# One modulation vector per VectorE product: transposed weights in place of accumulated products and folds

## The chip, the cores and the metric

The kernel runs on one core of one Trainium2 chip. The metric is the device time of one execution in microseconds (us). The core has a matrix engine (PE, TensorE), a vector engine (DVE, VectorE), an activation engine (ACT, ScalarE), GpSimd (POOL), a queue engine (SP, SyncE) that here issues nearly all weight loads, and DMA engines that move data between HBM and the on-chip SBUF. Each engine works through its own queue in order; semaphores tie the queues together.

## What is computed

One layer of a hybrid backbone over 256 latent and 256 context tokens of width 2048. Six modulation vectors come from the conditioning vector c, and two of them for the context too:

```python
mod_x = jnp.split((jax.nn.silu(c) @ w_mod[l] + b_mod[l])[:, None, :], 6, axis=-1)
mod_c = jnp.split((jax.nn.silu(c_ctx) @ w_mod[l] + b_mod[l])[None, None, :], 6, axis=-1)
...
x = x + mod_x[2] * merge_branches(o_attn, o_gla, rb, gate_a, gate_b, ...)
x = x + mod_x[5] * conv_ffn(modulate(x, g_ffn[l], mod_x[3], mod_x[4]), ...)
```

`w_mod` is 2048 x 12288 in float32: six parts of 2048 columns. Parts 0 and 1 (shift and scale ahead of the mixers) are needed for latent and context tokens, at the very start. Parts 2, 3, 4 and 5 are needed for the latent tokens alone and later: part 2 gates the mixers' output, 3 and 4 modulate the input of the feed-forward part, 5 gates its output. This case is about those four, 16.8 million products in all.

Around them stand the input projection (2048 x 13344), a windowed attention, a gated linear attention (GLA), two output projections, the merge, `w_out`, and a feed-forward part (FFN) with an up projection to 11264, a convolution, a gate and a down projection.

## The kernel before

**Weights.** All large products go through `proj_nat`, `proj_T` and `proj_pair`. A step of these (a chunk) takes 256 rows by 512 columns of a weight matrix: one load of 512 KB by SP (`load`, line 104) into a buffer `raw`, of which there are seven (pool `wr`); a rounded copy `whi` on ScalarE (line 227) and the remainder `wlo` on VectorE (line 228), with three buffers each; then the matmuls (line 83). So a chunk's split can run up to three chunks ahead of the matmuls that read it, and its load up to seven buffers ahead of the split. `tick()` runs at the head of every chunk. It calls what was deferred (`defer`), a step of GLA or attention (`beside`), and as many background steps (`bg_steps`) as `bg_rate` allows per chunk.

**Parts 0 and 1** are products on PE (`mod_both`): a load of 1 MB `mraw` from `w_mod`, matmuls into `pm`, a transpose, a product with `sel` into `pcol`.

**Parts 2 to 5** are the background steps of `mod_latent` (line 365), done on VectorE beside the weight products. For each part and each block j of 512 outputs there are eight steps. A step loads 256 rows by 512 columns of `w_mod` into a buffer of the same ring `raw` (the load of the next step is issued too), and adds the two products of a row block with its column of silu(c), `ccol`, onto `macc`, 128 x 512:

```python
i0 = V.scalar_tensor_tensor(a[0], raw[:, k, :], ccol[:, kt:kt + 1], a[0],
                            op0=ALU.mult, op1=ALU.add).ins
```

The first of the sixteen products of a block is a `tensor_scalar` (line 387), the other fifteen are line 391. After the eighth step the sums over the 128 partitions are still to be taken: a transpose within 32 x 32 blocks into `mtr` (line 397), a reduction to `mrs` (line 399), and, three chunks later or at a fixed place, a product with `sel` on PE (`pcl`, through `mm_b`, line 95, in float32), four copies of 32 partitions from PSUM (line 407) and the addition of the bias (line 409). `mm_b` ties such a product to the place in PE's order where it is called.

The first call (line 864) makes parts 3, 4 and 2, 96 steps: at 0.3 steps a chunk during the second key block and three value blocks of the GLA branch, 1.6 during the attention's key and value blocks, none during the query blocks and the attention, and 0.52 from the block `RB` through the merge. The second call (line 1190) makes part 5, 32 steps at 0.36 a chunk beside the first six of eleven blocks of the up projection; its `pcl` products are collected in `sums` and placed at the head of a block's first half (`up_banks`) or ahead of the down projection.

**Order.** Within an engine the order of the queue is not simply that of the program: work that waits for nothing moves ahead of work that does. Where the order matters it is tied by hand (`in_order`, no semaphore): the products of `mod_latent` come after the last `wlo`, the first of the second call after the last modulated tile of the FFN's input. The loads are tied to program order only up to `chain.clear()`, at the end of the opening part.

**The opening.** c is loaded as 16 rows of 128 into `crow`, passed through silu (line 126), turned on PE (line 133) and copied to `cS` (line 135) and `ccol` (line 136). `crow`, the rows of the small weight columns (`rows`, line 143, loaded by POOL) and the diagonal tiles `dg` (line 496) share two buffers, tag `t128`.

Of the kernel before, what the change touches and what calls it, by code (L numbers as in the profile page):

```python
# [8 lines left out]
F32 = mybir.dt.float32  # L9
# [3 lines left out]
ALU = mybir.AluOpType  # L13
AX = mybir.AxisListType
PSUM = bass.MemoryType.PSUM

P = 128
D = 2048
T = 256
KT = D // P  # L20
# [10 lines left out]
def layer_kernel(ctx, tc, A, out):  # L31
    nc = tc.nc
    V, S, G, PE = nc.vector, nc.scalar, nc.gpsimd, nc.tensor

    pool = lambda *a, **k: ctx.enter_context(tc.tile_pool(*a, **k))
    cst = pool(name="cst", bufs=1)
    big = pool(name="big", bufs=16)
    wr = pool(name="wr", bufs=7)
    wh = pool(name="wh", bufs=3)
    f2 = pool(name="f2", bufs=1)  # L40
    sm = pool(name="sm", bufs=4)
# [3 lines left out]

    w_in = A["w_in"][0]
    w_mod = A["w_mod"][0]
    F2_BUFS = {"fa": 4, "fb": 4, "fc": 6, "mod": 2}

    def M(name, shape, dt=F32):  # L50
        return big.tile(shape, dt, name=name, tag="M")
# [1 line left out]
    def W2(tag, name, shape, dt=F32):  # L53
        return f2.tile(shape, dt, name=name, tag=tag, bufs=F2_BUFS[tag])

    def bank(name, shape=(P, 512), side=False):

        return ps.tile(list(shape), F32, name=name, tag="side" if side else "main", bufs=3 if side else 1)
# [5 lines left out]
    def in_order(*ins):  # L64

        for a, b in zip(ins, ins[1:]):
            tc.add_manual_dep(b, a.name, mybir.DependencyInfo(
                mybir.DependencyClass.NoSync, mybir.DependencyReason.DATA), reason="order")
# [25 lines left out]
    def mm_b(*a, **k):  # L94
        return pe_seq(after(PE.matmul(*a, **k)))  # L95
# [6 lines left out]
    def load(dst, src):  # L102

        d = nc.sync.dma_start(dst, src).ins
        if chain and chain[-1] is None:
            chain[:] = [d]
        elif chain:
            tc.add_manual_dep(d, chain[-1].name, mybir.DependencyInfo(
                mybir.DependencyClass.NoSync, mybir.DependencyReason.DATA), reason="order of loads")
            chain[:] = [d]  # L110
        return d
# [16 lines left out]
        S.preload_act_table_set("natural_log_exp_and_others")  # L128
    cS = W2("fb", "cS", [P, KT, 32])
    V.memset(cS, 0.0)  # L130
    ccol = cst.tile([P, KT], F32, name="ccol")
    pt = bank("pc0", (P, 32))
    PE.transpose(pt, crow, ident[:32, :32])
    for i in range(2):
        V.tensor_copy(cS[:, :, i], pt[:, 16 * i:16 * i + 16])
    V.tensor_copy(ccol, pt[:, 0:16])

    def columns(name, parts, eng=G, put=None):
        rows = sm.tile([P, P], F32, name="rows", tag="t128", bufs=2)
# [23 lines left out]
    bg_steps = []  # L163
# [5 lines left out]
    def defer(n, fn):  # L169

        later.append([n, fn])
# [37 lines left out]
    def wload(src):  # L209
        n = src.shape[0] // P  # L210
        raw = wr.tile([P, 2, 512], F32, name="raw", tag="raw")
        load(raw[:, 0:n, :], src.rearrange("(c p) d -> p c d", p=P))
        return raw
# [148 lines left out]
        steps = [lambda k0=k0: step(k0) for k0 in range(0, KT, nk)]  # L362
        return steps if put is not None else steps + [end]

    def mod_latent(parts, put=lambda fn: defer(3, fn), begin=None):


        seq = [(part, dst, j, k0) for part, dst in parts for j in range(4) for k0 in range(0, KT, 2)]
        raws, a = {}, []

        def get(i):
            if i < len(seq) and i not in raws:
                part, _, j, k0 = seq[i]
                c0 = part * D + j * 512
                raws[i] = wload(w_mod[k0 * P:k0 * P + 256, c0:c0 + 512])

        def step(i):
            part, dst, j, k0 = seq[i]
            get(i)
            get(i + 1)  # L380
            if k0 == 0:
                a[:] = [W2("mod", "macc", [P, 512])]
            raw = raws[i]
            for k in range(2):
                kt = k0 + k
                if kt == 0:
                    i0 = V.tensor_scalar(a[0], raw[:, 0, :], ccol[:, 0:1], None, op0=ALU.mult).ins
                    if begin is not None:
                        in_order(begin, i0)
                else:  # L390
                    i0 = V.scalar_tensor_tensor(a[0], raw[:, k, :], ccol[:, kt:kt + 1], a[0],  # L391
                                                op0=ALU.mult, op1=ALU.add).ins
                if k == 0:
                    in_order(last_lo[0], i0)
            if k0 == KT - 2:
                tr = W2("mod", "mtr", [P, 16, 32])
                V.transpose(tr.rearrange("p a c -> p (a c)"), a[0])
                rs = sm.tile([P, 16], F32, name="mrs", tag="mrs", bufs=2)
                V.tensor_reduce(rs, tr, op=ALU.add, axis=AX.X)

                def out():
                    pc = bank("pcl", (32, 16))
                    mm_b(pc, sel[:, 0:32], rs, start=True, stop=True)
                    pv = pc.rearrange("p (a b) -> p b a", b=4)
                    d = dst[:, 4 * j:4 * j + 4]
                    for b4 in range(4):
                        V.tensor_copy(d[32 * b4:32 * b4 + 32, :], pv[:, b4, :])
                    b0 = part * 16 + j * 4
                    V.tensor_tensor(d, d, bmod[:, b0:b0 + 4], op=ALU.add)

                put(out)

        return [lambda i=i: step(i) for i in range(len(seq))]

    def rows_from_cols(name, col):

# [762 lines left out]
    pairs = []  # L1179
# [6 lines left out]
    in_order(pairs[0][0], *[i for kt in range(1, KT) for i in (pairs[kt][0], pairs[kt - 1][1])], pairs[-1][1])  # L1186
    in_order(small[-1], pairs[0][0])
    hold.extend([None, None] + [pairs[2 * c + 1][1] for c in range(2, 8)])
    sums = []
    bg_steps.extend(mod_latent([(5, gcol2)], sums.append, pairs[-1][1]))  # L1190
    bg_rate[:] = [0.36, 0.0]

    def up_banks(side):

        if side == 0:
            while sums:
                defer(3, sums.pop(0))
            return [acc.tile([P, 512], F32, name="acc", tag="acc") for _ in range(4)]
        return [bank("accs", side=(f > 0)) for f in range(4)]

# [2 lines left out]
    for half, blocks in enumerate((range(0, 6), range(6, 11))):  # L1203
        n = len(blocks)
        ah = [M("ah", [P, 8, T], F32R) for _ in range((n + 1) // 2)]
        al = [M("al", [P, 8, T], F32R) for _ in range((n + 1) // 2)]
        for i, j in enumerate(blocks):
            u = [[W2("fc", "u", [P, 2, T]) for _ in range(2)] for _ in range(2)]

            def up_evac(f, b, side, j=j, u=u, i=i, ah=ah, al=al):  # L1210
                p_ = f // 2
                uu = u[side][p_]
                d = uu[:, f % 2, :]
                fi = side * 44 + j * 4 + f
                us = W2("fa", "us", [P, T])
                S.activation(us, b[:, T:2 * T], AF.Copy)
                V.tensor_tensor(us, b[:, 0:T], us, op=ALU.add)
                S.activation(d, us, AF.Identity, scale=cw1[:, fi:fi + 1], bias=cb[:, fi:fi + 1])
                V.scalar_tensor_tensor(d[:, 1:T], us[:, 0:T - 1], cw0[:, fi:fi + 1], d[:, 1:T],
                                       op0=ALU.mult, op1=ALU.add)  # L1220
                V.scalar_tensor_tensor(d[:, 0:T - 1], us[:, 1:T], cw2[:, fi:fi + 1], d[:, 0:T - 1],
                                       op0=ALU.mult, op1=ALU.add)
                if f % 2 == 0:
                    return
                if side == 0:
                    S.activation(uu, uu, AF.Silu)
                else:
                    V.tensor_tensor(uu, uu, u[0][p_], op=ALU.mult)
                    q = slice((i % 2) * 4 + 2 * p_, (i % 2) * 4 + 2 * p_ + 2)
                    split(ah[i // 2][:, q, :], al[i // 2][:, q, :], uu)  # L1230

            for side in range(2):
                proj_pair(w_up, side * DFF + j * 512, ALL, lambda kt: h2[kt // 4][:, kt % 4, :, :],
                          up_banks(side), lambda f, b, side=side: up_evac(f, b, side))
        if half == 0:
            assert not bg_steps
            while sums:
                sums.pop(0)()
            flush()
            gate2 = rows_from_cols("gate2", gcol2)  # L1240
        ends = []
        for j in range(4):
            def dn_evac(t, b, j=j, half=half, gate2=gate2):
                js = slice(j * 512, (j + 1) * 512)
                y = W2("fc", "yd", [P, 512])
                a_ = V.tensor_tensor(y, b, gate2[:, js], op=ALU.mult).ins  # L1246
                if half == 0:
                    V.tensor_tensor(x1[t][:, js], x1[t][:, js], y, op=ALU.add)
                else:
                    if j == 3:  # L1250
                        in_order(*ends, a_)
                    ends[:] = [V.tensor_tensor(y, x1[t][:, js], y, op=ALU.add).ins]  # L1252
                    nc.sync.dma_start(out[0, t * P:(t + 1) * P, js], y)

            proj_nat(w_down, blocks[0] * 512, j * 512, list(range(n * 4)), [tok(ah, al, 0), tok(ah, al, 1)],
                     dn_evac, by_tile=(half == 1 and j == 3))
# [52 lines left out]
```

## Time and profile before

| what | value |
|---|---|
| time before, median of 3 runs | 2007.79 us (2007.24 to 2007.8) |
| span of the profiled execution, first to last instruction | 2005.1 us |
| left around the span, against the median | 2.7 us |
| mean granted TensorE clock | 0.999 |
| instructions | 27521 |
| busy: PE, PE's weight loads, DVE, ACT, POOL | 1977.6, 1645.9, 1435.7, 960.5, 45.0 us |
| read from HBM | 409.63 MB, 205 GB/s over the span |

The profiled execution gives its span; its own time is not listed beside the three timed runs, so the span plus the 2.7 us is taken as its time. How to read it: an engine's busy time is the sum of its instructions' durations with overlaps counted once; matmuls overlap, so a matmul's duration (about 390 ns at 512 columns) is longer than the distance from one to the next. A group row gives line, engine, operation, output and inputs, shapes, count, then busy time and mean duration of one, then the idle time of that engine just ahead of the group and what ended it. A row of the timeline gives start, duration from the first start to the last end, engine, line, operation, names, shapes and count. A row of the windows gives the window's length, the busy time (and instructions) of each engine in it, the granted clock, the busy share of the DMA engines and their rate.

### The profile page before, as it was taken

Reading aid. Unit: us, or ns where it says so; the run is one execution under the profiler, and the core shown is the slowest. Engines: PE = TensorE matmul, PEld = TensorE weight load, DVE = VectorE, ACT = ScalarE, POOL = GpSimd, SP = SyncE. Lnnn points to the kernel's source line nnn. Section 1 sums busy time; section 2 is a strip of 40 time slices with the busy share of each in tenths; the row PEclk is TensorE's granted clock in tenths of the full one; section 3 lists DMA queues with packets and bytes.
Section 4 is the critical chain, followed back from the end, with each engine's and each line's share of the span. In section 5 each row is a group of like instructions: output and inputs, shape, how many; then the busy total and the mean of one; then the engine's idle time right before and its main releaser. Section 6 shows DMA issues by size and latency. Waiting matters only on the chain.

```text
span 2005.1 us, 27521 instructions
## 1 busy us (share of the span) xinstructions
PE 1977.6 (99%) x10450; PEld 1645.9 (82%) x10450; DVE 1435.7 (72%) x2241; ACT 960.5 (48%) x1395; POOL 45.0 (2%) x66
## 2 busy tenths in 40 slices
PE   7999999999999999999999999999999999999999
PEld 5679888888877777888888888888888888888887
DVE  5666667877858888978876455898887555667754
ACT  4323464562345655444444444655555334555532
POOL 1000010011000000000000000000000000000000
PEclk9999999999999999999999999999999999999999
DMA  9986222326754456888886665587876656666563
GB/s 338 386 295 187 86 84 74 104 78 215 222 171 114 126 173 197 286 287 289 286 283 230 233 208 189 170 292 255 257 240 218 215 191 190 189 189 189 190 213 113
DMA packets 214149, 413.56 MB, mean 206 GB/s; under 512 B 12420, under 2 KB 20884, under 8 KB 212992
## 3 DMA queue, kind: packets, MB, share of 16 engines
q1 hardware_dynamic: 212464, 406.96, 63.4%
q0 software_dynamic: 1488, 4.82, 0.8%
q8 instruction: 82, 1.34, 0.3%
q14 instruction: 51, 0.42, 0.1%
q10 hardware_dynamic: 64, 0.02, 0.0%
HBM read 409.63 MB, written 2.11 MB: 205 GB/s over the span
## 4 chain that ended last, share of the span: by engine, by line
PE 60%; issue 16%; DVE 0%; POOL 0%; ACT 0%; DMA 0%; DVEq 0%; POOLq 0%
PE acc L83 47%; PE accs L83 12%; PE pto L98 0%; POOL att L913 0%; DMA glan<-in_gla_norm 0%; PE ptx L98 0%; POOL att L911 0%; PE pcl L95 0%; DVE yd L1252 0%; DVE yd L1246 0%; ACT yo L1128 0%; ACT whi L227 0%; ACT x1T L1136 0%; DVE og L1059 0%; DVE dg L1169 0%
## 5 line engine op out<-in xcount | busy, mean ns | idle before, releaser
L227 ACT ACTIVATE whi<-raw 128x1024 fp32r<-128x1024 f32 x568 | 601.5, 1059 | 814.6 <-PE acc L83 635.4
L228 DVE TENSOR_TENSOR wlo<-raw,whi 128x1024 fp32r<-128x1024 f32 x568 | 693.8, 1223 | 406.3 <-ACT whi L227 345.8
L391 DVE SCALAR_TENSOR_TENSOR macc<-raw,ccol,macc 128x512 f32<-128x512 f32 x240 | 179.8, 749 | 3.8
L83 PE MATMUL acc<-h,whi 128*128 128x512 f32 x704 | 176.9, 393 | 0.6 <-DVE h L523 0.6
L83 PE MATMUL accs<-h,whi 128*128 128x512 f32 x704 | 176.3, 392 | 0.0
L83 PEld LDWEIGHTS acc<-h,whi 128*128 128x128 f32 x704 | 126.5, 189 | 23.7 <-DVE h L523 0.9
L83 PEld LDWEIGHTS accs<-h,whi 128*128 128x128 f32 x704 | 126.6, 189 | 22.6
L83 PE MATMUL acc<-whi,h00hi 128*128 128x512 f32 x352 | 140.4, 399 | 1.0 <-DVE val L62 0.5
L83 PE MATMUL acc<-whi,h01hi 128*128 128x512 f32 x352 | 140.2, 398 | 0.0
L83 PE MATMUL acc<-whi,h00lo 128*128 128x512 f32 x352 | 138.4, 393 | 0.0
L83 PE MATMUL acc<-whi,h01lo 128*128 128x512 f32 x352 | 138.0, 392 | 0.0
L83 PE MATMUL acc<-whi,al 128*128 128x512 f32 x352 | 137.1, 389 | 0.0
L83 PE MATMUL acc<-whi,ah 128*128 128x512 f32 x352 | 137.0, 389 | 0.0
L83 PEld LDWEIGHTS acc<-h,wlo 128*128 128x128 f32 x704 | 96.2, 190 | 7.0
L83 PEld LDWEIGHTS accs<-h,wlo 128*128 128x128 f32 x704 | 96.0, 190 | 6.9
L83 PE MATMUL acc<-wlo,h01hi 128*128 128x512 f32 x352 | 98.6, 395 | 0.0
L83 PE MATMUL acc<-h,wlo 128*128 128x256 f32 x704 | 98.3, 282 | 0.0
L83 PE MATMUL accs<-h,wlo 128*128 128x256 f32 x704 | 98.2, 282 | 0.0
L83 PE MATMUL acc<-wlo,h00hi 128*128 128x512 f32 x352 | 97.8, 394 | 0.0
L83 PE MATMUL acc<-wlo,ah 128*128 128x512 f32 x352 | 94.5, 389 | 0.0
L83 PEld LDWEIGHTS acc<-whi,h00hi 128*128 128x128 f32 x352 | 66.4, 189 | 16.5 <-DVE val L62 1.0
L83 PEld LDWEIGHTS acc<-whi,ah 128*128 128x128 f32 x352 | 66.1, 188 | 13.6
(393 smaller groups left out, 3473.3 us busy)
## 6 DMA issues: line engine op xcount, KB each, us to landing
raw<-in_w_in SPq DMA_DIRECT2D x208, 512.0 KB, 4.5
raw<-in_w_up SPq DMA_DIRECT2D x176, 512.0 KB, 4.3
raw<-in_w_mod SPq DMA_DIRECT2D x128, 512.0 KB, 4.5
raw<-in_w_down SPq DMA_DIRECT2D x88, 512.0 KB, 3.7
mraw<-in_w_mod SPq DMA_DIRECT2D x32, 1024.0 KB, 13.4
raw<-in_w_attn_o SPq DMA_DIRECT2D x32, 512.0 KB, 4.9
raw<-in_w_gla_o SPq DMA_DIRECT2D x32, 512.0 KB, 5.1
raw<-in_w_out SPq DMA_DIRECT2D x32, 512.0 KB, 3.7
```

The source lines that it names most:

```text
L83: r = pe_seq(PE.matmul(*a, **k))
L227: j = S.activation(hi[:, 0:n, :], raw[:, 0:n, :], AF.Copy).ins
L228: i = V.tensor_tensor(lo[:, 0:n, :], raw[:, 0:n, :], hi[:, 0:n, :].bitcast(F32), op=ALU.subtract).ins
L391: i0 = V.scalar_tensor_tensor(a[0], raw[:, k, :], ccol[:, kt:kt + 1], a[0], op0=ALU.mult, op1=ALU.add).ins
```

## The change

`mod_latent` no longer adds up products along the rows of `w_mod`. The host hands in parts 2 to 5 transposed (`w_modT`, outputs on partitions), cut so that each load of 512 KB is one contiguous block: 128 outputs by 1024 inputs. `w_mod` itself keeps only parts 0 and 1, so its rows are 4096 columns long and no longer 12288.

silu(c) is written once to DRAM (`csd`, by a DMA on POOL's queue, issued ahead of the loads of `rows` in the program). For each half of the 2048 inputs, 1024 values of it are spread over all partitions into `csrow`, a single buffer of 4 KB a partition (it takes the place of the two buffers of `macc` and `mtr`), by a load on SP's queue. A step is then one `tensor_tensor_reduce`: 128 x 1024 products and their sum along the row, which lands as 128 finished values in one column of the destination, started from the bias in the first half of the inputs and from the first half's sum in the second. The order of the steps is half by half: all outputs of all parts with the first 1024 inputs, then all with the second. The number of steps that load weights stays 96 and 32; each call gets four more background steps (two loads of `csrow`, two empty steps behind them). The transposes, the reductions, the `pcl` products and the copies and additions behind them go, and so does `ccol`. The second call runs at 0.42 steps a chunk and not 0.36; the other rates stay. Context lines are left out below.

```diff
-    ccol = cst.tile([P, KT], F32, name="ccol")
+    csd = dram.tile([KT, P], F32, name="csd")
+    G.dma_start(csd, crow[0:16, :])
...
-    V.tensor_copy(ccol, pt[:, 0:16])
...
+        seq = [(part, dst, h, j) for h in range(2) for part, dst in parts for j in range(KT)]
+        raws, row = {}, []
         def get(i):
+            if 0 <= i < len(seq) and i not in raws:
+                part, _, h, j = seq[i]
+                raws[i] = wr.tile([P, 2, 512], F32, name="raw", tag="raw").rearrange("p a b -> p (a b)")
+                load(raws[i], A["w_modT"][part - 2, h, j])
+        def half(h):
+            row[:] = [f2.tile([P, 1024], F32, name="csrow", tag="mod", bufs=1)]
+            load(row[0], csd[8 * h:8 * h + 8, :].rearrange("k p -> (k p)").partition_broadcast(P))
         def step(i):
             get(i)
             get(i + 1)
+            d = dst[:, j:j + 1]
+            b0 = part * 16 + j
+            i0 = V.tensor_tensor_reduce(out=raws[i], in0=raws[i], in1=row[0], scale=1.0,
+                                        scalar=d if h else bmod[:, b0:b0 + 1],
+                                        op0=ALU.mult, op1=ALU.add, accum_out=d).ins
+            in_order(last_lo[0], i0)
+        n = len(seq) // 2
+        idle_ = lambda: None
+        return ([lambda: half(0), idle_] + [lambda i=i: step(i) for i in range(n)]
+                + [lambda: half(1), idle_] + [lambda i=i: step(i) for i in range(n, 2 * n)])
...
-    bg_rate[:] = [0.36, 0.0]
+    bg_rate[:] = [0.42, 0.0]
...
-            while sums:
-                defer(3, sums.pop(0))
...
+    data["w_modT"] = w_mod[0, :, 2 * D:].T.reshape(4, KT, P, 2, 1024).transpose(0, 3, 1, 2, 4)
+    data["w_mod"] = w_mod[:, :, :2 * D]
```

More of the change, by code (lines that the diff above doesn't have):

```diff
@@ L47, in layer_kernel @@
     w_mod = A["w_mod"][0]
-    F2_BUFS = {"fa": 4, "fb": 4, "fc": 6, "mod": 2}
+    F2_BUFS = {"fa": 4, "fb": 4, "fc": 6}
     def M(name, shape, dt=F32):
@@ L363, in mod_both, with mod_latent @@
         return steps if put is not None else steps + [end]
-    def mod_latent(parts, put=lambda fn: defer(3, fn), begin=None):
-        seq = [(part, dst, j, k0) for part, dst in parts for j in range(4) for k0 in range(0, KT, 2)]
-        raws, a = {}, []
+    def mod_latent(parts, begin=None):
+        seq = [(part, dst, h, j) for h in range(2) for part, dst in parts for j in range(KT)]
+        raws, row = {}, []
         def get(i):
[L372 to L375, printed above, removed]
+            if 0 <= i < len(seq) and i not in raws:
[5 more added lines that the diff above has]
+            load(row[0], csd[8 * h:8 * h + 8, :].rearrange("k p -> (k p)").partition_broadcast(P))
@@ L377, in step @@
         def step(i):
-            part, dst, j, k0 = seq[i]
+            part, dst, h, j = seq[i]
             get(i)
             get(i + 1)
[L381 to L411, printed above, removed]
@@ L413, in mod_latent @@
-        return [lambda i=i: step(i) for i in range(len(seq))]
+            d = dst[:, j:j + 1]
[3 more added lines that the diff above has]
+                                        op0=ALU.mult, op1=ALU.add, accum_out=d).ins
+            if begin is not None and i == 0:
+                in_order(begin, i0)
+            in_order(last_lo[0], i0)
@@ L1188, in layer_kernel @@
     hold.extend([None, None] + [pairs[2 * c + 1][1] for c in range(2, 8)])
-    sums = []
-    bg_steps.extend(mod_latent([(5, gcol2)], sums.append, pairs[-1][1]))
-    bg_rate[:] = [0.36, 0.0]
+    bg_steps.extend(mod_latent([(5, gcol2)], pairs[-1][1]))
+    bg_rate[:] = [0.42, 0.0]
     def up_banks(side):
         if side == 0:
-            while sums:
-                defer(3, sums.pop(0))
             return [acc.tile([P, 512], F32, name="acc", tag="acc") for _ in range(4)]
@@ L1236, in layer_kernel @@
             assert not bg_steps
-            while sums:
-                sums.pop(0)()
             flush()
@@ L1297 @@
     data = {n: inputs[n] for n in _INS}
+    w_mod = np.asarray(data["w_mod"])
+    data["w_modT"] = w_mod[0, :, 2 * D:].T.reshape(4, KT, P, 2, 1024).transpose(0, 3, 1, 2, 4)
+    data["w_mod"] = w_mod[:, :, :2 * D]
     data.update(_consts())
```

## The prediction

> **What bounds the kernel now.** I read the busy times of the page first, then the windows by stage, then the list of PE's waits. Busy time and instructions stand behind each engine; in the windows, PE, PE's weight loads, DVE, ACT and POOL follow the length, then clock, DMA share and rate.
>
> ```profile
> span 2005.1 us, 27521 instructions
> PE 1977.6 (99%) x10450; PEld 1645.9 (82%) x10450; DVE 1435.7 (72%) x2241; ACT 960.5 (48%) x1395; POOL 45.0 (2%) x66
> ...
> 0.00:150.00 150.00, 136.20 (x1035) 101.62 (x1036) 91.91 (x203) 49.88 (x77) 7.87 (x19) 0.99 0.96 340
> 200.00:600.00 400.00, 395.42 (x2157) 330.18 (x2155) 295.83 (x539) 190.54 (x358) 29.69 (x36) 1.00 0.43 129
> 800.00:1250.00 450.00, 450.00 (x2028) 370.50 (x2027) 315.27 (x376) 197.57 (x214) 1.62 (x3) 1.00 0.77 255
> 1300.00:1550.00 250.00, 250.00 (x1418) 218.74 (x1418) 219.65 (x332) 142.50 (x204) 0.00 (x0) 1.00 0.78 253
> ```
>
> PE is busy 1977.6 of 2005.1 us at full clock. Of its 27.5 us of idle, 13.8 lie in the first 150 us, ahead of any step of `mod_latent`; 4.6 lie between 200 and 600, where steps run beside GLA and the attention's keys; where most steps run (800 to 1250, 1300 to 1550) there are none. So VectorE's time is worth nothing by itself. Two things can move the end: fewer or dearer instructions on PE, and waits of PE that come or go.
>
> **What goes from PE.** The folds end in a float32 product with `sel` on PE, sixteen times, two matmuls each. Their busy time misleads, since matmuls overlap; I read what such a pair does to the distance between chunks, in a block with two token tiles and in an up block (start, duration, ..., count).
>
> ```profile
> 1035.78 0.39 PE L83 MATMUL acc<-whi,h00hi 128*128 128x512 f32 x1
> ...
> 1038.59 0.23 PE L95 MATMUL pcl<-mrs,sel 128*32 128x16 f32 x2
> 1038.76 0.50 PE L83 MATMUL acc<-whi,h00hi 128*128 128x512 f32 x1
> ...
> 1041.61 0.39 PE L83 MATMUL acc<-whi,h00hi 128*128 128x512 f32 x1
> ...
> 1044.33 0.39 PE L83 MATMUL acc<-whi,h00hi 128*128 128x512 f32 x1
> ```
>
> ```profile
> 1404.36 2.00 PE L83 MATMUL acc<-h,whi 128*128 128x512 f32 x8
> 1407.16 2.00 PE L83 MATMUL acc<-h,whi 128*128 128x512 f32 x8
> ...
> 1410.04 0.24 PE L95 MATMUL pcl<-mrs,sel 128*32 128x16 f32 x2
> ...
> 1413.10 0.40 PE L83 MATMUL acc<-h,whi 128*128 128x512 f32 x1
> ```
>
> The chunk from 1041.61 to 1044.33 has no such pair and lasts 2.72 us. The two from 1035.78 to 1041.61 last 5.83, so the pair between them costs 5.83 - 5.44 = 0.39 us, more than its own 0.23: the next matmul follows late too (0.50 instead of 0.39). In the up block a plain chunk lasts 1407.16 - 1404.36 = 2.80 and the two around a pair 1413.10 - 1407.16 = 5.94, so 0.34. I take 0.37 for 14 of the 16. Two stand next to other float32 products (turnings of the mixers' tiles), which delay the next matmul anyway; between 0 and 0.37 I give them 0.2. Sum: 14 x 0.37 + 2 x 0.2 = **5.6 us** less on PE. Bounds: 16 x 0.16 = 2.6 (only the 0.16 from one pair's start to the next matmul's) and 16 x 0.39 = 6.2. Nothing hides this: PE has no idle there.
>
> **What VectorE does instead.** Rows of the groups: busy time, mean ns of one, idle ahead.
>
> ```profile
> L228 DVE TENSOR_TENSOR wlo<-raw,whi 128x1024 fp32r<-128x1024 f32 x568 | 693.8, 1223 | 406.3 <-ACT whi L227 345.8 <-ACT gm L740 24.8 <-PE acc L83 24.4
> L391 DVE SCALAR_TENSOR_TENSOR macc<-raw,ccol,macc 128x512 f32<-128x512 f32 x240 | 179.8, 749 | 3.8
> L989 DVE CUSTOM_DVE_ANT_0 s<-pS,att 128x512 f32<-128x512 f32 x32 | 20.6, 686 | 1.1 <-PE pS L95 1.1
> L397 DVE STREAM_TRANSPOSE mtr<-macc 128x512 f32<-128x512 f32 x16 | 11.4, 710 | 0.4
> L399 DVE TENSOR_REDUCE mrs<-mtr 128x16 f32<-128x512 f32 x16 | 10.9, 680 | 0.2
> L407 DVE COPY gcol<-pcl 32x4 f32<-32x4 f32 x32 | 4.8, 151 | 1.0 <-PE pcl L95 0.2
> L473 DVE SCALAR_TENSOR_TENSOR vb<-x 128x2048 f32<-128x2048 f32 x2 | 4.6, 2287 | 1.2 <-DMA x<-in_ctx 1.2
> L989 DVE DVE_READ_ACCUMULATOR2_ANT mx<- 128x1 f32 x32 | 2.6, 83 | 0.0
> ```
>
> Out: 179.8 + 11.4 + 10.9 and 64 copies of 0.151 (9.7) = 211.8 us, 1.65 a step (the first, cheaper product of each block is left out). In: 128 products with a sum over 1024. The attention's operation of this kind takes 686 at 512, as a plain two-operand product does; the two-operand row at 1024 is 1223, and the readout 83, so 1.31 a step, 167 us. The bounds are 1.31 and a doubled pass, 2 x 1.223 + 0.083 = 2.53. I take 1.31, by the row of 2048 with a sum (2287, no second pass). VectorE so loses some 45 us, worth **0** as PE does not wait for it in the busiest stages. [...]
>
> Some waits of PE do hang on VectorE:
>
> ```profile
> PE pm L95 <- DMA mraw<-in_w_mod: 3.6, 3, 1.8
> PE pa L95 <- DVE q L785: 2.2, 3, 1.0
> ...
> 295.15 0.74 DVE L391 SCALAR_TENSOR_TENSOR macc<-raw,ccol,macc 128x512 f32<-128x512 f32 x1
> 297.02 0.74 DVE L391 SCALAR_TENSOR_TENSOR macc<-raw,ccol,macc 128x512 f32<-128x512 f32 x1
> 298.75 1.16 PE L95 MATMUL pa<-q,kb 128*128 128x128 f32 x8 [0.97 <-DVE q L785]
> ```
>
> Ahead of the wait at 298.75 two pieces of 0.74 lay in VectorE's queue in front of GLA's chain. Afterwards it is one piece of 1.31 there, which can fall before or behind. I count 0, between -2.2 (the wait for q vanishes) and +2 (four heads times the 0.57 by which one piece is longer).
>
> **What is added.** (a) `csd` on POOL's queue, and it waits for silu(c). (The last three rows are DMA issues: count, size, us to landing.)
>
> ```profile
> 3.45 0.57 POOL L908 DMA_DIRECT2D sink<-in_attn_sink  x1
> 6.44 0.31 ACT L126 ACTIVATE crow<-crow 32x128 f32<-32x128 f32 x1
> 13.06 0.27 PE L98 MATMUL pt_c<-ident,rows 128*128 128x128 f32 x1
> 14.84 1.07 PE L95 MATMUL pm<-mraw,cS 128*32 128x256 f32 x16 [1.51 <-DMA mraw<-in_w_mod]
> ...
> raw<-in_w_up SPq DMA_DIRECT2D x176, 512.0 KB, 4.3
> raw<-in_w_attn_o SPq DMA_DIRECT2D x32, 512.0 KB, 4.9
> rows<-in_g_ffn POOLq DMA_DIRECT2D x1, 8.0 KB, 6.1
> ```
>
> Silu ends at 6.75. POOL already issued line 908's load at 3.45, hundreds of program lines early, because it waited for nothing; so `csd` most likely moves behind the three loads of `rows`, at no cost. If it stays ahead of them, the last of them is issued at 6.75 + 4 x 0.5 = 8.8, and lands at about 15 by the 6.1 us of its present flight; PE then turns `rows` at 15, past the 14.84 at which it stops for `mraw` anyway, and waits for `mraw` again later. So 0, at most +1. `dg` on `crow`'s buffer now waits for this DMA too; by the flight above it has landed at 6.75 + 0.5 + 6.1 = 13.4, before PE takes up at 14.84 the products that stand ahead of `dg`'s. (b) `w_mod`'s rows become 16 KB instead of 48 KB apart. Loads from rows 45 KB apart (`w_up`) land after 4.3 us, from rows 8 KB apart (`w_attn_o`) after 4.9, in another stage; I count 0, between -2.1 and +2.1 (0.6 of 4.3, on the 14.84 us at which the first `mraw` is used), while PE waits 3.6 us in all for `mraw`. (c) Four loads of `csrow`, 512 KB on SP's queue beside some 700 others; the second of each call waits until the last product of the first half has read the buffer. That is the first rival. (d) 0.42 instead of 0.36 steps a chunk in the up blocks: 6% of a chunk's 512 KB more on a DMA share of 0.78, and 0.42 x 1.31 = 0.55 us of VectorE per chunk instead of 0.36 x 1.65 = 0.59. Hidden.
>
> Sum against the profiled execution: 2005.1 - 5.6 = 1999.5 span, plus the 2.7 between span and median: **2002.2 us**, 0.28% less. About 0.2% (4 us) is what a measurement here can tell from no change, so the forecast lies just past that.
>
> **Rivals.**
>
> First, *the saving is given back by the load queue.* While SP stands at `csrow`'s second load, weight loads stand behind it.
>
> ```profile
> 821.08 1.50 SPq L104 DMA_DIRECT2D raw<-in_w_attn_o  x2
> 835.09 0.39 PE L83 MATMUL acc<-whi,oh 128*128 128x512 f32 x1
> ...
> 1113.04 0.46 SPq L1107 DMA_DIRECT2D x<-in_x  x1
> 1123.50 0.37 SPq L104 DMA_DIRECT2D raw<-in_w_gla_o  x1
> ```
>
> A weight load is issued 14.0 us ahead of its first matmul; landing (4.9) and splitting (1.22 on VectorE, ScalarE's copy taken alike) need 7.3, so 6.7 are spare. The load of `csrow` comes two chunks (5.4 us) behind the last product of the first half, and takes about 2.1 itself at that stage's 255 GB/s. 5.4 + 2.1 = 7.5 is 0.8 past the spare time, and a product that falls a chunk late adds 2.7: up to 3.5 us, at two places, once in each call. Against it: line 1107's load stood at 1113 ahead of the `w_gla_o` loads that precede it in the program, so SP's order follows readiness. With some of the waits above it gives 2002.2 + 4 = **2006 us**.
>
> Second, on the other side: *VectorE becomes the bound in the up blocks*, because a step holds it longer than its rows say, in a doubled pass or at the head of its queue. Between 1300 and 1550 it idles 250 - 219.65 = 30.4 us. That stretch has 250 / 2.80 = 89.3 chunks; 32.1 steps of 1.65 (53.0 us) go and 37.5 come, so it decides from (53.0 + 30.4) / 37.5 = 2.22 us a step. At 2.53 (94.9 us) the stretch overflows by 11.5. In the attention's key and value blocks (24 matmuls a chunk, 5.44 us) the row below leaves 4.7 us idle; 9.2 chunks at 1.6 steps, 0.88 dearer each, take 12.9: 8.2 over. Sum +20: **2022 us**. [...]
>
> ```profile
> 500.00:550.00 50.00, 50.00 (x230) 40.52 (x229) 45.26 (x91) 15.89 (x28) 0.00 (x0) 1.00 0.72 222
> ```
>
> Third, *the GLA waits vanish too*: 2002.2 - 2.2 = **2000 us**.
>
> **Chances.** Forecast 0.55; third rival 0.05; first 0.24; second 0.16, since the operation is seen only with a PSUM source and a piece of 1.31 us cannot be interrupted. Faster by over 0.2% is the first two, 0.60; within 0.2% 0.24; slower 0.16. The range leaves out the second rival and little else: from 2007.8 - 6.2 - 2.2 - 2.1 = 1997.3 (all bounds that help) to 2007.8 - 5.6 + 7 + 2 = 2011.2 (the first rival at 3.5 us twice, and GLA's upper bound), rounded to 1997.5 and 2011.
>
> **What would show it.** Right: no `pcl` on PE; PE's busy time down by 4 to 6 us and its idle time still 27 to 28; the new operation at about 1.2 us with a readout of 0.08; VectorE down by about 45 to 50 us; chunks of 2.72 and 2.80 all through. Wrong: waits of `acc` for `wlo` or `whi` at the middle of a call (first rival); a step near 2.4 us and VectorE full in the up blocks (second); `pm` or `pt_c` later than 14.84 in the opening.

## The result and the profile after

The changed kernel takes 2002.34 us (median of 9 runs, 2002.04 to 2002.61), the kernel before 2007.77 (9 runs, 2006.49 to 2008.46). The ratio is 0.9973, with a 95% interval of 0.9964 to 0.9983. The forecast was 2002.2.

The spans of the two profiled executions are 2005.1 and 2000.3 us, 4.8 apart. First the page of the changed kernel, with the windows of the stages that were shown of before (length, busy time of PE, PE's weight loads, DVE, ACT and POOL, clock, DMA share, rate).

```profile
span 2000.3 us, 27285 instructions
PE 1972.3 (99%) x10418; PEld 1645.9 (82%) x10418; DVE 1385.3 (69%) x2128; ACT 961.1 (48%) x1395; POOL 46.9 (2%) x67
...
0.00:150.00 150.00, 134.72 (x1008) 101.06 (x1012) 88.61 (x197) 49.22 (x76) 6.12 (x15) 0.97 0.94 334
200.00:600.00 400.00, 395.87 (x2159) 331.92 (x2158) 280.22 (x507) 191.39 (x358) 31.35 (x36) 1.00 0.40 128
800.00:1250.00 450.00, 450.00 (x2027) 372.46 (x2026) 299.44 (x336) 199.03 (x216) 1.62 (x3) 1.00 0.77 259
1300.00:1550.00 250.00, 250.00 (x1414) 219.01 (x1413) 206.98 (x305) 140.83 (x201) 1.06 (x2) 1.00 0.77 260
```

PE has 32 matmuls less (10418 for 10450) and 5.3 us less busy time; its idle time is 28.0 us for 27.5. VectorE is 50.4 us down. The busiest stages still show no idle of PE. One thing in these rows does not fit the forecast: in the first 150 us PE is busy 134.72 us for 136.20 at a clock of 0.97 for 0.99, although nothing of `mod_latent` runs there.

The groups and chunks that answer to those of before are the new operation with its readout, and three chunk starts where a pair of float32 products used to stand:

```profile
L387 DVE CUSTOM_DVE_ANT_0 raw<-raw,csrow,c 128x1024 f32<-128x1024 f32 x64 | 81.2, 1284 | 0.0
L387 DVE DVE_READ_ACCUMULATOR2_ANT gcol<- 128x1 f32 x64 | 5.4, 84 | 0.0
```

```profile
1033.95 0.39 PE L83 MATMUL acc<-whi,h00hi 128*128 128x512 f32 x1
...
1036.67 0.39 PE L83 MATMUL acc<-whi,h00hi 128*128 128x512 f32 x1
...
1039.39 0.39 PE L83 MATMUL acc<-whi,h00hi 128*128 128x512 f32 x1
```

A step holds VectorE 1.28 + 0.08 = 1.36 us, and both chunks last 2.72.

To see where the time went I set the same matmul of both executions side by side, from the timelines of PE. The first column is its start before; the others are how much earlier (-) or later (+) it starts in the changed kernel and in experiment e1 below.

| PE takes up | before, us | changed | e1 |
|---|---|---|---|
| the first `pm` of the opening | 14.84 | +2.86 | -1.01 |
| the first weight product | 27.87 | +3.54 | -0.97 |
| the low-rank product `plr`, after the opening | 209.29 | +3.38 | -1.29 |
| the attention's key block (from 464.58) | 464.58 | +2.01 | -2.64 |
| the merge's first `w_attn_o` block | 835.09 | -0.28 | -5.06 |
| the output projection | 1168.10 | -2.64 | -7.41 |
| the up blocks | 1267.03 | -2.75 | -7.52 |
| the second half of the up blocks | 1667.80 | -4.51 | -9.27 |

So the changed kernel **loses 3.4 us in the opening and gains 7.9 us behind it**. The forecast's size was met by luck: a gain of over 5.6 and a loss that it did not have stand against each other.

The loss is plain in the queue that issues the loads. SP's first entries, first of the changed kernel, and what PE does meanwhile:

```profile
1.19 0.90 SPq L104 DMA_DIRECT2D x<-in_x  x2
9.88 0.33 SPq L104 DMA_DIRECT2D csrow<-csd  x1
10.26 7.25 SPq L104 DMA_DIRECT2D mraw<-in_w_mod  x4
...
12.89 0.27 PE L98 MATMUL pt_c<-ident,rows 128*128 128x128 f32 x1
17.70 1.93 PE L95 MATMUL pm<-mraw,cS 128*32 128x256 f32 x16 [4.54 <-DMA mraw<-in_w_mod]
```

The kernel before has, at the same place in SP's queue:

```profile
1.19 0.89 SPq L104 DMA_DIRECT2D x<-in_x  x2
2.12 12.58 SPq L104 DMA_DIRECT2D mraw<-in_w_mod  x4
```

The first load of `csrow`, which the program issues beside the GLA branch, has moved up in SP's queue, to right behind the two loads of `x`: its buffer was free from the start. It waits there for `csd`, which POOL issues at 6.83 once silu is done and which takes 3.0 us to land, and all loads of `mraw` stand behind it from 2.1 to 10.3 us. PE then waits 4.54 us for the first `mraw` instead of 1.51.

### The profile page after: what moved, and what is told of

Read it like the earlier page. It is cut to its first block, busy times and chain, and to the rows that moved or that the text cites. A ratio compares the mean times of both kernels' runs of the same rounds, so it can differ in the third digit from the quotient of the medians.

```text
span 2000.3 us, 27285 instructions
## 1 busy us (share of the span) xinstructions
PE 1972.3 (99%) x10418; PEld 1645.9 (82%) x10418; DVE 1385.3 (69%) x2128; ACT 961.1 (48%) x1395; POOL 46.9 (2%) x67
## 3 DMA queue, kind: packets, MB, share of 16 engines
HBM read 411.73 MB, written 2.12 MB: 207 GB/s over the span
## 4 chain that ended last, share of the span: by engine, by line
PE 59%; DVE 0%; ACT 0%; issue 0%; DVEq 0%
PE acc L83 47%; PE accs L83 12%; PE pto L98 0%; PE ptx L98 0%; DVE yd L1231 0%; DVE yd L1225 0%; ACT yo L1112 0%; ACT whi L227 0%; ACT x1T L1120 0%; DVE dg L1153 0%; ACT h L506 0%; DVE h L507 0%; DVE x1T L505 0%; PE pr L1155 0%; DVE fac L1150 0%
## 5 line engine op out<-in xcount | busy, mean ns | idle before, releaser
L228 DVE TENSOR_TENSOR wlo<-raw,whi 128x1024 fp32r<-128x1024 f32 x568 | 694.5, 1224 | 448.2 <-ACT whi L227 406.9
L387 DVE CUSTOM_DVE_ANT_0 raw<-raw,csrow,c 128x1024 f32<-128x1024 f32 x64 | 81.2, 1284 | 0.0
```

Of the source, the lines that this page charges most:

```text
L228: i = V.tensor_tensor(lo[:, 0:n, :], raw[:, 0:n, :], hi[:, 0:n, :].bitcast(F32), op=ALU.subtract).ins
L387: i0 = V.tensor_tensor_reduce(out=raws[i], in0=raws[i], in1=row[0], scale=1.0, scalar=d if h else bmod[:, b0:b0 + 1], op0=ALU.mult, op1=AL ...
```

## The experiments

The theory after the result had three parts: SP's queue was held in the opening (3.4 us lost); the sixteen pairs on PE are worth 5.6 to 6.0; some 2 us more came from VectorE. All times are medians with 5 or more runs; the kernel before was run beside each set and gave 2006.8 to 2007.2 us. Kernels are compared by these times and by their profiles.

### e1: the first load of csrow behind the opening's loads

```diff
+    opened = list(chain)
     chain.clear()
...
-            load(row[0], csd[...].partition_broadcast(P))
+            d = load(row[0], csd[...].partition_broadcast(P))
+            if begin is None and h == 0:
+                in_order(opened[0], d)
```

> The changed kernel, with the first load of csrow tied behind the last load of the opening; the same work. Theory (this load stands in SP's queue from 2 us to 9.9 us waiting for csd, and the mraw loads stand behind it): pm starts at about 14.8 us again instead of 17.7, time down by 3.4 us, 1999 us. Rival (the opening is later because the rows of w_mod lie 16 KB apart): pm stays at about 17 to 18 us, 2002.3 us.

Measured: 1997.71 us, ratio 0.9955 (0.9941 to 0.9968). SP issues `mraw` at 2.12 again and `csrow` at 161.9. Of e1, SP's queue and PE's first products on `mraw`:

```profile
1.18 0.90 SPq L104 DMA_DIRECT2D x<-in_x  x2
2.12 11.52 SPq L104 DMA_DIRECT2D mraw<-in_w_mod  x4
...
13.83 1.07 PE L95 MATMUL pm<-mraw,cS 128*32 128x256 f32 x16 [1.22 <-DMA mraw<-in_w_mod]
16.76 1.94 PE L95 MATMUL pm<-mraw,cS 128*32 128x256 f32 x16 [1.86 <-DMA mraw<-in_w_mod]
```

The 4.6 us between the medians of e1 and the changed kernel hold the 3.4 and about 1 us by which the opening differs from one set of runs to another (`pm` starts at 13.8 to 14.8 in the kernels that do not hold the queue). Each against the kernel before of its own set, e1 is 9.2 us faster and the changed kernel 5.4, so 3.8 apart. This version beats both kernels.

### e2: the same load from POOL's queue

```diff
+            src = csd[...].partition_broadcast(P)
+            if begin is None and h == 0:
+                G.dma_start(row[0], src)
+            else:
+                load(row[0], src)
```

> The changed kernel, with the first load of csrow issued from POOL's queue instead of SP's; it still runs in the opening. Theory (SP's queue is held): SP issues mraw at 2 us, about 1999 us, at most 1.5 us above e1 if the 512 KB take DMA time from mraw. Rival (it is the 512 KB more in a stage where the DMA engines are full, not the queue): pm as late as in the changed kernel, 2002 us.

Measured: 1999.78 us (0.9964, 0.9951 to 0.9976). The load still runs in the opening (POOL issues it at 14.36), `pm` starts at 14.42, and the kernel is 2.1 us above e1. By matched matmuls the opening ends 3.0 us earlier than in the changed kernel and 1.7 later than in e1, so the queue was the larger part of the loss. What the 512 KB more cost in the opening is not settled: PE's waits for `mraw` sum to 5.3 us here and to 3.1 in e1, but to 2.8 to 4.3 in the other kernels without a `csrow` load there. Another 1 us of the distance to e1 lies behind the attention, where `pto` waits 1.8 us for `sr` and 1.0 in e1.

### e3: the kernel before without the products on PE

```diff
-                    pc = bank("pcl", (32, 16))
-                    mm_b(pc, sel[:, 0:32], rs, start=True, stop=True)
-                    pv = pc.rearrange("p (a b) -> p b a", b=4)
+                    pv = rs.rearrange("p (a b) -> p b a", b=4)
```

> The kernel before, without the sixteen products with sel on PE (the sum over the four blocks of 32 partitions is left out; the copies and the bias read mrs directly). Theory (each pair costs PE 0.37 us, two of them less): 5.6 to 6.0 us less, 2002 us. Rival (PE's saving is only the 0.16 us from the pair to the next matmul, and the change gains by VectorE's relief): 2.6 us less, 2005 us.

Measured: 2001.4 us (0.9972, 0.9962 to 0.9983), 5.5 us less, with VectorE's work all but unchanged (1434.5 us busy for 1435.7). The rival is out: a pair costs PE about 0.35 us and not 0.16. Waits of PE for VectorE moved too (1.7 us for 0.4 at `v3l`, 0.2 for 0.9 at `kf`), so the median alone would not settle it; by matched matmuls PE gains 0.3 to 0.4 at the places of the pairs one by one.

### e4: the kernel before with w_mod's rows 16 KB apart

```diff
+    data["w_mod4"] = w_mod[0, :, 2 * D:]
+    data["w_mod"] = w_mod[:, :, :2 * D]
```

(`mod_latent` reads `w_mod4`.)

> The kernel before, with w_mod handed in as two arrays: parts 0 and 1 with rows 16 KB apart, parts 2 to 5 with rows 32 KB apart. Theory (the distance of the rows does not matter): within 0.5 us of 2007.8. Rival (it delays mraw, and with it the opening): 2 to 3.5 us more, 2010 to 2011 us.

Measured: 2006.23 us (0.9997, 0.9988 to 1.0006). The distance of the rows makes no difference that shows.

### e5, e6, e7: VectorE's time per step

Each is e1 with more VectorE work behind every step:

```diff
+            V.tensor_tensor(raws[i][:, 0:128], raws[i][:, 0:128], row[0][:, 0:128], op=ALU.mult)
```

for e5, and for e6 and e7, with n = 512 and 1024,

```diff
+            V.tensor_tensor_reduce(out=raws[i][:, 0:n], in0=raws[i][:, 0:n], in1=row[0][:, 0:n], scale=1.0,
+                                   scalar=0.0, op0=ALU.mult, op1=ALU.add, accum_out=spare)
```

> e1 with one more VectorE product of 128 columns (about 0.29 us) behind each of the 128 steps, so that a step holds VectorE for about 1.65 us as before the change; the product overwrites weights already used. Theory (VectorE's relief itself took away about 2 us of waits of PE beside GLA and behind the attention): about 2 us above e1, 1999.7 us. Rival (VectorE's time is worth nothing, as the prediction had it): e1's time within 0.5 us, 1997.7 us.

> e1 with a second product with a sum over 512 columns behind each step (its sum is thrown away), so about 2.13 us of VectorE a step, below the 2.22 us at which the up blocks were reckoned to become VectorE-bound. By the reckoning of the second rival: nothing in the up blocks, 2 to 3 us in the attention's key and value blocks, some 2 us of waits as in e5: 2001 to 2003 us. If VectorE's queue counts well before it is full: over 2006 us.

> e1 with the whole product done twice in each step (the second sum is thrown away), so about 2.72 us of VectorE a step, above the 2.22 us. By the reckoning of the second rival: 37.5 x 2.72 - 83.4 = 18.6 us over in the up blocks, 14.7 x (2.72 - 1.65) - 4.7 = 11 us in the attention's key and value blocks: about 30 us above e1, 2027 us. If VectorE has more slack than reckoned: under 2010 us.

Measured: e5 1997.7 us (0.9954, 0.9942 to 0.9967), the time of e1; e6 1998.73 (0.9958, 0.9946 to 0.9971); e7 2010.66 (1.0019, 1.001 to 1.0028). So in the sum the time per step is worth nothing up to the old 1.65 us and about 1 us at 2.13. Doubled products cost 13 us and not 30.

The equal time of e5 is a balance, though. By matched matmuls e5 is 0.3 us behind e1 at the end of the opening, 1.4 from 470 to 700 us, and level (0.1) from the merge on. PE's wait for `kf` in the GLA, first of the kernel before, then of e5 (e1 and the changed kernel have none):

```profile
PE pa L95 <- DVE kf L823: 0.9, 2, 0.7
...
PE pa L95 <- DVE kf L811: 1.3, 2, 1.0
```

And the first turnings of the mixers' tiles (`pto`), first of e1, then of e5:

```profile
794.16 1.23 PE L98 MATMUL pto<-ident,sr 128*128 128x128 f32 x8 [1.02 <-DVE sr L1047]
...
792.54 0.63 PE L98 MATMUL pto<-ident,sr 128*128 128x128 f32 x4
794.28 0.63 PE L98 MATMUL pto<-ident,sr 128*128 128x128 f32 x4
```

The longer step brings the wait for `kf` back, and about as much is made up behind the attention, where `pto` no longer waits. So VectorE's relief per step did take a wait away; that it adds nothing to the end time is what this order of the work shows, and no run shows why the rest made it up.

The stretch from 1280 to 1530, of e1 first and of e7 below:

```profile
1280.00:1530.00 250.00, 250.00 (x1432) 219.79 (x1430) 208.09 (x310) 141.98 (x205) 0.00 (x0) 1.00 0.80 261
```

```profile
1280.00:1530.00 250.00, 244.97 (x1386) 212.82 (x1385) 234.58 (x362) 134.26 (x194) 0.00 (x0) 1.00 0.77 248
```

PE idles here for the first time, 5.0 us, while VectorE is at 234.6 of 250. By matched matmuls e7 falls 8.7 us behind e1 between 1345 and 1505, 7.2 of them from 1371 on. Taken from e1's own row, the reckoning is 208.1 + 37.5 x 1.36 = 259, 9 us over, near the 8.7; the forecast had counted too much other work there (250 - 83.4 = 166.6 us and not 208.1 - 51 = 157.1). Another 3.4 us were lost before that beside the GLA, where PE waits 3.5 us for `kf`. In the attention's key and value blocks almost nothing was lost (0.3 us between 470 and 700), although VectorE is busy 88.1 of the 90 us from 470 to 560. That the lead of the splits over the matmuls took up the backlog there is a reading that no run tested.

### e8: no wait on SP for the second half

```diff
-                + [lambda: half(1), idle_] + [lambda i=i: step(i) for i in range(n, 2 * n)])
+                + [idle_, idle_] + [lambda i=i: step(i) for i in range(n, 2 * n)])
```

> e1 without the second load of csrow in each call (the second half of the inputs is multiplied by the first half's values), so nothing on SP's queue waits for the last product of the first half. Theory (weight loads have enough lead, the wait on SP costs PE nothing): e1's time within 0.5 us, 1997.7 us. First rival (the weight loads behind that wait come late): 1 to 7 us below e1.

Measured: 1998.3 us (0.9957, 0.9945 to 0.9969), 0.6 us above e1 and not below. Of the profiled executions e8 loses 0.8 us more at a wait of `pto` for `sr`, 1.9 us for 1.0. In e1 the load stands in the queue until the last product has read the buffer, and PE does not wait for a weight load or a split near either place. The first rival had its place right and no price.

### e9: the folds' bursts on VectorE put back

```diff
+            if i % 8 == 7:
+                V.transpose(raws[i][:, 512:1024], raws[i][:, 0:512])
+                rs = sm.tile([P, 16], F32, name="mrs", tag="mrs", bufs=2)
+                V.tensor_reduce(rs, raws[i][:, 512:1024].rearrange("p (a c) -> p a c", c=32), op=ALU.add, axis=AX.X)
...
```

(with the four copies and the addition, onto a spare tile)

> e1 with the VectorE part of the old folds put back behind every eighth step (transpose, reduction, four small copies, one addition, about 2 us in a row, on spare data; nothing on PE). e1 gained some 2 us more than 16 pairs explain. If the folds' bursts on VectorE were behind these 2 us: 1999 to 2000 us. If not: e1's time within 0.5 us, 1997.7 us.

Measured: 2003.14 us (0.9979, 0.9971 to 0.9988), 5.4 above e1, more than either theory had. It is nearly all at one place: by matched matmuls 7.1 us are lost between 455 and 480, and 1 us comes back behind the attention. PE's waits of e9, the matmul that waited, and VectorE's queue just before:

```profile
PE acc L83 <- DVE v3l L62: 4.9, 1, 4.9
...
464.00 1.30 DVE L389 CUSTOM_DVE_ANT_0 raw<-raw,csrow,c 128x1024 f32<-128x1024 f32 x1
465.24 0.40 DVE L401 TENSOR_TENSOR spare<-spare,mrs 128x4 f32<-128x4 f32 x1
465.56 1.42 DVE L389 CUSTOM_DVE_ANT_0 raw<-raw,csrow,c 128x1024 f32<-128x1024 f32 x1
466.91 0.68 DVE L62 TENSOR_TENSOR atc<-pa,atc 128x512 fp32r<-128x512 f32 x1
467.52 1.21 DVE L228 TENSOR_TENSOR wlo<-raw,whi 128x1024 fp32r<-128x1024 f32 x1
468.65 2.47 DVE L62 TENSOR_TENSOR v3l<-acc,v3h 128x512 fp32r<-128x512 f32 x4
469.38 0.80 PE L83 MATMUL acc<-whi,h00hi 128*128 128x512 f32 x1 [4.94 <-DVE v3l L62]
```

`v3l` empties the accumulators at the end of the last GLA value block; the next block cannot start until it has read them. In e1 it starts at 464.09 and PE waits 0.7 us:

```profile
463.48 0.68 DVE L62 TENSOR_TENSOR atc<-pa,atc 128x512 fp32r<-128x512 f32 x1
464.09 0.68 DVE L62 TENSOR_TENSOR v3l<-acc,v3h 128x512 fp32r<-128x512 f32 x1
464.82 0.50 PE L83 MATMUL acc<-whi,h00hi 128*128 128x512 f32 x1 [0.69 <-DVE v3l L62]
```

The wait is 4.2 us longer; the other 3 us of the 7.1 come behind it, with the clock. This is the row of e9 from 470 us (length, PE busy, clock, DMA share, rate); up to 475 us its matmuls of 512 columns start 0.43 us apart and not 0.23:

```profile
470.00:473.00 3.00, 3.00 (x9) 0.50 0.76 277
```

What counted here is what stood ahead of the evacuation when it was due (from 464.00 to 468.65 us two steps, an addition, `atc` and a `wlo`), not VectorE's sum: e6 added 88 us of products to that and cost about 1 us. The kernel before had the same bursts and waited 0.4 there: its fold happened to lie elsewhere. So e9 shows a hazard, not where the 2 us came from.

### e10: the products on PE put back into e1

```diff
+            if i % 8 == 7:
+                mv = row[0][:, 0:16]
+                def out():
+                    pc = bank("pcl", (32, 16))
+                    mm_b(pc, sel[:, 0:32], mv, start=True, stop=True)
+                put(out)
...
```

(with `put` and `sums` as in the kernel before)

> e1 with the sixteen products with sel put back on PE at their old places in the order (on spare data, nothing reads them; nothing added on VectorE). By 0.37 us each and less for those beside other float32 products: 5.6 to 6.0 us above e1, 2003.5 us. If the 2 us more come with the pairs too (PE's order around them): 7.5 to 8 us above e1, 2005.5 us. If e3's gain came from elsewhere: under 2.6 us above e1.

Measured: 2003.46 us (0.9982, 0.9973 to 0.9991), 5.75 above e1. By matched matmuls the opening is level and each pair shows as a step of 0.3 to 0.4 us. With e3, taken from the other side, the pairs are settled at 5.5 to 5.8 us.

## Why the prediction was right, and where it was not

**The saving on PE** (5.6 us, 0.37 a pair) was right, both in size and in how it was read: from the distance between chunk starts, not from the 0.19 us that a matmul of the pair lasts. e3 gives 5.5, e10 5.75. In the changed kernel the matched matmuls step by 0.29 to 0.41 us at the sixteen places, 5.9 in all. The 0.2 for the two beside turnings was too low: they step by 0.31 and 0.36.

**The new operation** was put at 1.31 us a step and measured 1.36; VectorE fell by 50.4 us for a forecast of 45 to 50. No run shows the doubled pass from which the second rival's 2.53 us was worked out: the operation took 1284 ns at 1024 elements out of SBUF, 686 at 512 with one source in PSUM, and 688 at 512 out of SBUF in e6. Row L473 of the kernel before, a scalar-tensor-tensor operation with a sum whose two sources are one float32 tile in SBUF, shows none either: it takes 2287 ns for 2048 columns, where the plain two-operand operation of row L228 takes 1223 for 1024.

**VectorE's relief counted as 0** came out right in the sum (e5). In the busiest stages PE indeed does not wait for VectorE (busy 450.00 of 450 us and 250.00 of 250 in the changed kernel). Beside the GLA it does, and there the prediction priced only the wait for `q`: with the longer step of e5 the wait for `kf` is back, and is made up behind the attention. The second rival's direction was right too: it decides near the point where VectorE is full (e7: 13 us, with VectorE busy 234.6 of 250). Its reckoning, carried over to e7, was twice too large: it summed too much other work in the up blocks, and the overflow reckoned for the attention's key and value blocks (11 us in the forecast of e7) did not appear. It was not priced that a burst ahead of a block's evacuation costs PE at once (e9: a wait of 4.94 us for 0.69).

**The GLA waits** stayed for `q` (2.3 us for 2.2) and went for `kf` (0.9). That and a regrouping of the turned tiles behind the attention (eight `pto` products together at 798.95, where before four stood at 791.57 and four at 793.97) go with the most of the 2 us beyond the pairs: by the matched matmuls 0.8 us come between 209 and 718 and 0.7 between 718 and 835. Both stay when the pairs are put back (e10). Neither stays when the steps are lengthened to the old 1.65 us (e5), and yet the time does. So the cause of these 2 us is open.

**The load queue** is the step that failed. The prediction's own sign of being wrong, `pm` later than 14.84, did show (17.70). Part (c) of the sum counted "four loads of `csrow`" and made a rival of the second of each call, in the middle of a call. That wait is there and costs nothing (e8). The first load was not costed at all. The prediction itself had shown that SP's order follows readiness (line 1107's load ahead of earlier ones) and used it as comfort; by the same fact a load with a free buffer had moved to the head of the queue, and there its other condition, `csd`, held everything behind it. Its price is 3.4 us by matched matmuls, and e1 wins it back. The other two sources offered for a late opening were priced soundly: `csd` moved behind `rows` and cost nothing, and the rows' distance costs nothing (e4).

So the forecast's 5.6 us was met by 5.9 from the pairs in this execution, some 2 more behind the opening, and 3.4 lost in it: 5.9 + 2.0 - 3.4 = 4.5 by the last matched blocks, 4.8 by the spans, 5.4 by the medians. The mechanism of the pairs was foreseen; that the time came out 0.1 us from the forecast was luck, since neither the 2 us nor the 3.4 stood in the sum.

## What to carry to other kernels

When a change adds a transfer, ask for each of its conditions separately when it is met: where the order of a queue goes by free buffers, as SP's did here, the transfer is taken up early, and the queue then stands at its data with everything behind it (the first `mraw` at 10.26 us and not at 2.12, 3.4 us lost). On an engine that is busy all the time, read what a small product costs from the distance between its neighbours' starts (0.35 us for a pair that is busy for 0.23). An engine off the path can be worth nothing in the sum (e5) and still sets the time wherever its queue is long just as an accumulator has to be emptied (e9, 5.4 us). An equal time after an experiment does not show that nothing moved: compare the waits as well (e5: 1.3 us for `kf`, none in e1).

## What the runs showed of the hardware

A float32 pair of 128x16 between weight products in the rounded format costs 0.35 us of PE where its own matmuls last 0.19 each (e3 and e10); at two places next to other float32 products it cost 0.31 and 0.36.

After two waits of over 4 us PE's clock was lower. In the changed kernel's opening, after 4.54 us without a matmul, sixteen `pm` products took 1.93 us where the kernel before took 1.07 after 1.51 us of waiting; in e9 the clock stood at 0.50 after the wait of 4.94 us. Shorter waits are no sure sign: the kernel before fell too, a little later, after waits of 1.51 and 1.83 us, and e1 after 1.22 and 1.86 (0.50 between 17 and 20 us), while e2 stayed at 1.00 after 1.42, 1.64 and 1.62. The granted clock, per 3 us, of the changed kernel's opening, then two rows of the kernel before (length, PE busy, clock, DMA share, rate):

```profile
14.00:17.00 3.00, 0.00 (x0) 0.70 1.01 342
17.00:20.00 3.00, 1.93 (x16) 0.50 1.10 352
20.00:23.00 3.00, 2.38 (x18) 0.50 1.10 348
23.00:26.00 3.00, 3.00 (x26) 0.59 1.10 355
26.00:29.00 3.00, 3.00 (x41) 1.00 1.06 398
...
17.00:20.00 3.00, 2.25 (x18) 0.62 1.09 348
20.00:23.00 3.00, 3.00 (x31) 0.81 1.08 360
```

The opening's delay grew from 2.86 us at `pm` to 3.54 at the first weight product, and it grew at one place, beside the longer stretch at the low clock: eight small products ahead of the weight products (`warm`) took 1.91 us (clock 0.59 from 23 to 26) where the kernel before took 1.29 (0.81 from 20 to 23). The slower `pm` products cost nothing, as the next wait for `mraw` was shorter by as much (0.99 us for 1.83).

PE was busy from 20.62 us on in the changed kernel, and its clock stood at 0.59 between 23 and 26 and at 1.00 from 26; rows of 3 us do not time the return more closely. What lowers the clock, and after how long a wait, no run here shows.
